# Token-major pieces on one PSUM bank of either pool, and longer pauses in the compression and the solve

## The chip, the cores and the metric

The kernel runs on one core of a Trainium2 chip. The time is that of the device for one execution, in microseconds (us); three executions give 573.76, 575.64 and 576.48, median 575.64. One more execution was profiled. The engines are PE (TensorE, the matmuls), PEld (its weight loads), DVE (VectorE), ACT (ScalarE), POOL (GpSimd) and SP (SyncE, which here only issues DMA transfers).

## The reference

One decoder layer for 256 tokens of width 2048. One input projection feeds eight heads of native sparse attention (NSA) and sixteen heads of RWKV-7 time mixing; their gated outputs go through one output projection, a norm and the residual. Cut to what matters here:

```python
def compress(kv, pos, w1, w2):          # called for k_cmp and for v_cmp
    idx = jnp.arange(n_cmp)[:, None] * CMP_STRIDE + jnp.arange(CMP_BLOCK)[None, :]
    blocks = kv[:, idx] + pos[None, None, :, None, :]
    flat = blocks.transpose(0, 1, 3, 2, 4).reshape(B, n_cmp, G, CMP_BLOCK * D)
    return jax.nn.silu(flat @ w1) @ w2  # w1 is 4096 x 128
...
h = x + RMSNorm_post( W_out( concat[ NSA_heads * silu(z_A), RWKV7_heads * silu(z_B) ] ) )
```

## The kernel before

Everything is unrolled. **Projection pieces** are the bulk of PE's work. Each takes a weight tile by DMA (L276, tile `rf...`, `rt...` or `ro...` for feature-major, token-major and output pieces), is split into a high half by ACT (L284, `hf`, `ht`, `ho`) and a low half by DVE (L285, `lf`, `lt`, `lo`), and is multiplied in three products: high by high and low of x, low by high. Most have 24 matmuls of 128x256 per weight tile. The two token-major pieces (function `token_major`, w = 0 and 1) instead use x as the stationary operand: each accumulates two token halves, 128x268 each, over six weight tiles, `pts` being the two PSUM banks; ACT empties them at L1073 (values) and L1074 (gates).

**Lanes** are generators that run beside the pieces: `rwkv`, `blk0`, `blk1`, `nsa0`, `nsa1`, `gate`, `chain`. A lane does a step and yields a number; it is continued when the planned PE time `now` has passed by that number. So the yields decide where in the written order a step stands. A scheduler with priorities (fetch before chain, evac, rwkv, mix, proj) then sets the final order of every engine from the written one, and the order is fixed at build time. The program waits on the chip where an operand isn't ready when its engine gets to it.

**PSUM** has eight banks. `ppool` owns banks 0 and 1 (NPP = 2) and serves the projection pieces in turn; `banks` owns the other six and serves the lanes. SBUF work space is one arena of 51 units of 256 columns, given out by first fit.

**Compression.** `compress` runs for kc and vc in lane nsa0. The 2 MB of w1 come in four quarters of 512 KB (tile `arena<-in_cw_dram`; L878 loads the first, L882 the next one). Each quarter feeds 8 matmuls of 128x128 with four small stationary tiles; the next-but-one quarter can only be loaded when a quarter's slot in the arena is free again.

**Solve.** For each half of the RWKV heads `solve` inverts 32x32 triangles on DVE (L672 and L674), sends the result Z and its transpose to DRAM (`zs`, `zt`, L680 and L681) and back into other partitions (L694 and L701), and multiplies corners of 32x32 with them (the corner products, on GR and ZT). A loop over four chunks follows; its last step is a group of 8 matmuls on VS and GR and 4 on AR (yp), and ends half 1. Then: ACT copies and squares (L813, L823), DVE reduces (L824), ACT takes a root (L827, with a table load), DVE scales (L828, L829), PE transposes 16 tiles of 64x64 (L164, ytp), DVE adds (L839).

**Output.** Output piece `ho`nj multiplies the mixed heads of index j into output columns n. j = 0 to 3 are NSA's (tile mixA), j = 4 to 7 RWKV's (mixB, split by ACT L1040 and DVE L1041 per half; it takes the place of GR, so it begins when the last yp has read GR). L1048 gates a head before the split.

The function that this change touches, as the profile's line numbers have them:

Of the kernel before, what the change touches and what calls it, by code (L numbers as in the profile page):

```python
# [117 lines left out]
def hybrid_block(ctx: ExitStack, tc: tile.TileContext, xT, xtok, wfm, wtm, wout, vecs, gpost, lora, table,  # L118
# [15 lines left out]
    @contextmanager  # L134
    def at(name):
        old, tc.cur_priority = tc.cur_priority, level[name]
        try:
            yield
        finally:
            level[name], tc.cur_priority = tc.cur_priority, old  # L140
# [6 lines left out]
    def mm(o, lhsT, rhs, **kw):  # L147
        n = 1
        for d_ in rhs.shape[1:]:
            n *= d_  # L150
        now[0] += n * (1 if rhs.dtype == F32R else 4) / 2400.0
        last[0] = PE.matmul(o, lhsT, rhs, **kw)  # L152
# [25 lines left out]
    banks = Pool(lambda a, k: banks_[:, NPP + a, :] if k == 1 else banks_[:, NPP + a:NPP + a + k, :], 8 - NPP, now)  # L178
    ppool = Pool(lambda a, k: banks_[:, a, :], NPP, now)

    def sb(k=1):
        while arena.find(k) is None:
            yield lambda: arena.find(k) is not None
        return arena.take(k)

    def bank():
        while banks.find(1) is None:
            yield lambda: banks.find(1) is not None
        return banks.take(1)
# [6 lines left out]
    def bank2():  # L196
        while banks.find(2, 2) is None:
            yield lambda: banks.find(2, 2) is not None
        return banks.take(2, 2)
# [24 lines left out]
    def progress():  # L224
        go = True
        while go:
            go = False
            for n in lanes:
                if can(n) and running[n][0] <= now[0]:
                    step(n)  # L230
                    go = True
                    break
# [8 lines left out]
    def until(cond):  # L241
        while not cond():
            wait()

    def pick(pool, k, step_=1):
        until(lambda: pool.find(k, step_) is not None)
        return pool.take(k, step_)
# [60 lines left out]
    def take():  # L308
        while queue and len(ready) < 4:
            fetch()  # L310
        return ready.pop(0)
# [225 lines left out]
    def block(A, hb, i, m):  # L537
        yield lambda: A.opened and A.normed[i]
        yield from rwkv_k(A, i, m)
        yield from rwkv_r(A, i, m)  # L540
        yield from rwkv_v(A, i, m)
        A.blocks += 1
        if A.blocks == 4:
            lanes["chain"].append(solve(hb))
# [103 lines left out]
    def solve(hb):  # L648
# [49 lines left out]
        for par in range(2):  # L698
            b0 = 64 * (1 - par)
            for a in range(2):  # L700
                SP.dma_start(ZT[b0:b0 + 32, :, a, :], ztv[0, par, :, :, a])  # L701
        yield 9.0
        t2p = yield from bank2()
        t2v = t2p[:, :, 0:T].rearrange("p b (j a s) -> p b j a s", j=4, a=2)
        for i in range(4):
# [153 lines left out]
    def compress(a, nm):  # L859
        if a == 0:  # L860
            SP.dma_start(post, pos)
            SP.dma_start(w2t, cw2)
        blks = yield from sb(4)
        blk = blks.ap.rearrange("p (j g i) -> p j g i", j=32, g=2)
        POOL.memset(blk[:, :, :, 15:16], 0.0)
        src = cT[nm].ap
        for g in range(2):
            w_g = bass.AP(tensor=src.tensor, offset=src.offset + g * T, ap=[src.ap[0], [1, 32], [16, 15]])
            DVE.tensor_tensor(blk[:, :, g, 0:15], w_g, post[:, a, :, None].to_broadcast([P, 32, 15]), op=ALU.add)
        cT[nm].free(2.0)  # L870
        yield 1.0
        cps = yield from bank()
        w1n = None
        for hf in range(4):
            w1 = w1n
            if w1 is None:
                w1 = yield from sb(4)
                SP.dma_start(w1[:], cw1[a, :, 8 * hf:8 * hf + 8, :].rearrange("p j d -> p (j d)"))  # L878
                yield 3.0
            if hf < 3:  # L880
                w1n = yield from sb(4)
                SP.dma_start(w1n[:], cw1[a, :, 8 * hf + 8:8 * hf + 16, :].rearrange("p j d -> p (j d)"))  # L882
            for j in range(2):
                for q in range(4):
                    jj = 4 * j + q
                    mm(cps[32 * q:32 * q + 32, 0:P], blk[:, 8 * hf + jj].rearrange("p g i -> p (g i)"),
                       w1[:, jj * P:jj * P + P], start=hf == 0 and j == 0, stop=hf == 3 and j == 1)
            w1.free(1.0)
            yield 2.0
        blks.free(1.0)  # L890
        csb = yield from sb()
        DVE.tensor_copy(csb[:, 0:P], cps[:, 0:P])
        cps.free(1.0)
        yps = yield from bank()
        mm(yps[:, 0:32], csb[:, 0:P], qsum, start=True, stop=True)
        csb.free(1.0)
        yh = tp.tile([P, 32], F32, tag="yh", name=f"yh{nm}")
        DVE.tensor_scalar(yh, yps[:, 0:32], 0.5, None, op0=ALU.mult)
        yps.free(1.0)
        yt = tp.tile([P, 32], F32, tag="yt", name=f"yt{nm}")  # L900
        ACT.activation(yt, yh, AF.Tanh)
        DVE.scalar_tensor_tensor(yh, yt, 1.0, yh, op0=ALU.add, op1=ALU.mult)
        yield 2.0
        ops = yield from bank()
        if a == 0:
            mm(ops[:, 0:32], w2t[:, a, :], yh, start=True, stop=True)
            for g in range(2):
                ACT.activation(KCH[:, g, 128:144], ops[:, 16 * g:16 * g + 16], AF.Copy)
                DVE.tensor_tensor(KCL[:, g, 128:144], ops[:, 16 * g:16 * g + 16], KCH[:, g, 128:144].bitcast(F32),
                                  op=ALU.subtract)  # L910
        else:
            for g in range(2):
                mm(ops[0:16, g * P:(g + 1) * P], yh[:, 16 * g:16 * g + 16], w2t[:, a, :], start=True, stop=True)
            opv = ops[0:16, 0:2 * P].rearrange("p (g d) -> p g d", g=2)
            ACT.activation(vcS[0:16], opv, AF.Copy)
            ACT.activation(vcS[64:80], opv, AF.Copy)
            DVE.tensor_tensor(vcS[32:48], opv, vcS[0:16].bitcast(F32), op=ALU.subtract)
        ops.free(2.0)
        ready_kv[nm] = True
        yield 0.4  # L920
# [132 lines left out]
    def token_major():  # L1053
        VV = N_.VV = pick(arena, 4).ap.rearrange("p (w i t) -> p w i t", w=2, i=2)
        for w in range(2):
            pts = [pick(ppool, 1) for i in range(2)]
            for hf in range(len(TMK) - 1):
                H, L = take()
                with at("proj"):
                    for part in range(2):  # L1060
                        for k in range(TMK[hf + 1] - TMK[hf]):
                            kk_ = TMK[hf] + k
                            for i in range(2):
                                xs = slice(i * P, (i + 1) * P)
                                if part == 0:
                                    mm(pts[i][:, 0:268], xH[:, kk_, xs], H[:, k, :], start=kk_ == 0, stop=False)
                                    mm(pts[i][:, 0:268], xL[:, kk_, xs], H[:, k, :], start=False, stop=False)
                                else:
                                    mm(pts[i][:, 0:268], xH[:, kk_, xs], L[:, k, :], start=False, stop=kk_ == NK - 1)
                progress()  # L1070
            with at("evac"):
                for i in range(2):
                    ACT.activation(VV[:, w, i, :], pts[i][:, 0:T], AF.Copy, scale=rst[:, i:i + 1])  # L1073
                    ACT.activation(gate[:, i, 12 * w:12 * w + 12], pts[i][:, T:268], AF.Tanh, scale=rsth[:, i:i + 1])  # L1074
                    pts[i].free(1.0)
        DVE.tensor_scalar(gate, gate, 0.5, 0.5, op0=ALU.mult, op1=ALU.add)
        ready_kv["tm"] = True
# [6 lines left out]
    for j, (nm, i) in enumerate(FM):  # L1084
        if j == N_PRE_TM:
            token_major()
# [27 lines left out]
        elif nm in ("kc", "vc"):  # L1114
# [5 lines left out]
            if i == 1:  # L1120
                lanes["nsa0"].append(compress(("kc", "vc").index(nm), nm))
# [45 lines left out]
    def out_part(n, js, pool, order=None):  # L1167
        pts = [pick(pool, 1) for i in range(2)]
        for pair in order or [[j] for j in js]:
            hl = [take() for j in pair]  # L1170
            for i in range(2):
                with at("proj"):
                    for j, (H, L) in zip(pair, hl):
                        out_mms(pts[i][:], i, H, L, j, j == js[0], j == js[-1])
            progress()
        return pts

    for n in range(NA):
        pts = out_part(n, range(4), ppool if n % 2 == 0 else banks)
# [51 lines left out]
    for n in range(4):  # L1231
# [7 lines left out]
        pts = out_part(n, js, ppool if n % 2 == 0 else banks, order)  # L1239
# [85 lines left out]
```

## Time and profile before

| | |
|---|---|
| three timed runs, median | 573.76, 575.64, 576.48 us; 575.64 us |
| the profiled execution's own time | 576.96 us |
| its span, first to last instruction | 575.2 us |
| PE busy, PEld busy | 557.7 us (97%), 522.1 us (91%) |
| DVE, ACT, POOL busy | 426.9 us (74%), 311.7 us (54%), 57.4 us (10%) |
| mean granted TensorE clock | 0.992 |

The span is what the trace covers; 1.76 us of the own time lie around it. Busy is the time in which an engine has an instruction in it. A matmul's end is modelled and overlaps the next one's start, so the distance from start to start says more than a duration. In a list by time, the square bracket behind an instruction gives the idle time ahead of it and what ended it.

### The profile page before, as it was taken

Reading aid. Unit: us, or ns where it says so; the run is one execution under the profiler, and the core shown is the slowest. Engines: PE = TensorE matmul, PEld = TensorE weight load, DVE = VectorE, ACT = ScalarE, POOL = GpSimd, SP = SyncE. Lnnn points to the kernel's source line nnn. Section 1 sums busy time; section 2 is a strip of 40 time slices with the busy share of each in tenths; the row PEclk is TensorE's granted clock in tenths of the full one; section 3 lists DMA queues with packets and bytes.
Section 4 is the critical chain, followed back from the end, with each engine's and each line's share of the span. In section 5 each row is a group of like instructions: output and inputs, shape, how many; then the busy total and the mean of one; then the engine's idle time right before and its main releaser. Section 6 shows DMA issues by size and latency. Waiting matters only on the chain.

```text
span 575.2 us, 12152 instructions
## 1 busy us (share of the span) xinstructions
PE 557.7 (97%) x4808; PEld 522.1 (91%) x4808; DVE 426.9 (74%) x885; ACT 311.7 (54%) x561; POOL 57.4 (10%) x97
## 2 busy tenths in 40 slices
PE   7999999999989999999998999999999999999993
PEld 7999999989989999999998999999999987778882
DVE  5989978859968765578759569999666566666755
ACT  7678656524436334476655667865543355645432
POOL 5103303300010000030102000000000000000002
PEclk9999999999989999999999999999999999999998
DMA  8796554477556734344256454434754446756624
GB/s 309 289 289 211 165 179 148 146 212 231 181 185 199 199 128 144 111 148 117 53 186 199 141 141 148 144 121 147 212 148 153 141 150 186 287 183 204 198 74 147
DMA packets 40789, 99.97 MB, mean 174 GB/s; under 512 B 14331, under 2 KB 17052, under 8 KB 40348
## 3 DMA queue, kind: packets, MB, share of 16 engines
q1 hardware_dynamic: 40444, 98.88, 53.9%
q8 instruction: 38, 0.62, 0.4%
q10 hardware_dynamic: 288, 0.31, 0.2%
q14 instruction: 19, 0.16, 0.1%
HBM read 93.93 MB, written 5.24 MB: 172 GB/s over the span
## 4 chain that ended last, share of the span: by engine, by line
PE 88%; DMA 5%; ACT 3%; SPq 1%; DVE 1%; issue 1%; POOL 0%; DVEq 0%; ACTq 0%; POOLq 0%
PE banks L152 86%; DMA arena<-in_cw_dram 2%; PE banks L164 2%; DMA xr<-in_xT_dram 1%; DMA arena<-zt 1%; SPq L694 1%; DMA zs<-arena 1%; DMA rt__3359<-in_wtm_dram 1%; DVE y L1222 0%; POOL xH L326 0%; ACT L559 0%; ACT L827 0%; SPq L276 0%; ACT hf__2850 L284 0%; ACT hf__3585 L284 0%
## 5 line engine op out<-in xcount | busy, mean ns | idle before, releaser
L152 PE MATMUL banks<-arena 128*32 128x128 f32 (+4 forms) x468 | 31.9, 256 | 3.0 <-DMA arena<-in_cw_dram 1.9
L152 PEld LDWEIGHTS banks<-arena 128*32 128x32 f32 (+3 forms) x468 | 26.4, 136 | 6.5 <-DMA arena<-in_cw_dram 2.6
L672 DVE TENSOR_TENSOR arena<-arena 64x31 f32<-64x31 f32 (+15 forms) x62 | 20.3, 328 | 6.3 <-DMA arena<-us 5.7
L674 DVE TENSOR_TENSOR arena<-arena 64x31 f32<-64x31 f32 (+15 forms) x62 | 20.5, 331 | 0.5
L473 ACT ACTIVATE small<-small 128x256 f32<-128x256 f32 x25 | 12.5, 507 | 14.9 <-DVE small L471 14.8
L164 PE MATMUL banks<-small,arena 128*128 128x128 f32 (+1 forms) x112 | 16.1, 262 | 0.0
L528 DVE RECIPROCAL arena<-arena 128x256 f32<-128x256 f32 x8 | 14.0, 1746 | 2.6 <-PE banks L152 2.6
L152 PE MATMUL banks<-AR,arena 64*128 64x128 f32 x128 | 14.3, 292 | 0.0
L1029 ACT ACTIVATE arena<-arena 128x256 f32<-128x256 f32 x16 | 6.6, 414 | 13.9 <-DVE arena L1141 9.8
L971 ACT ACTIVATE arena<-arena,mx 128x128 f32<-128x128 f32 (+1 forms) x32 | 14.1, 444 | 0.0
L558 POOL TENSOR_SCALAR arena<-arena 128x256 f32<-128x256 f32 x8 | 8.6, 1076 | 54.7 <-ACT arena L557 51.6
L164 PEld LDWEIGHTS banks<-small,arena 128*128 128x128 f32 (+1 forms) x112 | 12.0, 140 | 1.9 <-issue 1.1
L152 PEld LDWEIGHTS banks<-AR,arena 64*128 64x128 f32 x128 | 11.4, 187 | 2.2 <-issue 0.8
L1226 POOL TENSOR_TENSOR y<-y,xres 128x512 f32<-128x512 f32 x2 | 2.9, 1453 | 105.0 <-ACT y L1225 105.0
L474 DVE SCALAR_TENSOR_TENSOR arena<-small 128x256 f32<-128x256 f32 x25 | 12.0, 480 | 1.0 <-ACT small L473 0.8
L621 DVE TENSOR_TENSOR GR<-banks,small 128x1024 f32<-128x1024 f32 x8 | 9.8, 1220 | 3.8 <-PE banks L152 3.7
L152 PE MATMUL banks<-VS,GR 128*64 128x64 f32 x256 | 11.4, 229 | 0.0
L561 POOL TENSOR_SCALAR arena<-arena,small 128x256 f32<-128x256 f32 x8 | 6.1, 757 | 50.9 <-ACT arena L559 50.8
L585 POOL COPY AR<-arena 128x4 f32<-128x4 f32 x8 | 8.6, 1078 | 24.7 <-DVE arena L575 24.7
L152 PEld LDWEIGHTS banks<-VS,GR 128*64 128x64 f32 x256 | 9.6, 137 | 1.7 <-issue 0.4
L795 POOL MEMSET arena<- 64x256 f32 x12 | 3.7, 307 | 69.1 <-PE banks L152 66.1
L471 DVE TENSOR_TENSOR small<-banks,small 128x256 f32<-128x256 f32 x25 | 10.3, 418 | 0.1
(1378 smaller groups left out, 2157.0 us busy)
## 6 DMA issues: line engine op xcount, KB each, us to landing
arena<-in_cw_dram SPq DMA_DIRECT2D x8, 512.0 KB, 6.2
xres<-in_xtok_dram SPq DMA_DIRECT2D x2, 1024.0 KB, 10.1
xr<-in_xT_dram SPq DMA_DIRECT2D x3, 512.0 KB, 9.0
bscr<-arena SPq DMA_DIRECT2D x1, 1536.0 KB, 8.7
out_dram<-y SPq DMA_DIRECT2D x5, 256.0 KB, 3.1
arena<-bscr SPq DMA_DIRECT2D x8, 128.0 KB, 2.9
gpt<-in_gpost_dram SPq DMA_DIRECT2D x1, 1024.0 KB, 6.8
rf__93<-in_wfm_dram SPq DMA_DIRECT2D x1, 512.0 KB, 4.7
```

The costliest lines, as they stand in the source:

```text
L152: last[0] = PE.matmul(o, lhsT, rhs, **kw)
L164: PE.transpose(out=o, in_=i, identity=idn)
L471: DVE.tensor_tensor(f[:, 1:T + 1], pt[:, :T], rbc, op=ALU.mult)
L473: ACT.activation(tm, f[:, 0:T], AF.Copy, scale=vcol(V_MU, c))
L474: DVE.scalar_tensor_tensor(o, f[:, 1:T + 1], omu[:, c:c + 1], tm, op0=ALU.mult, op1=ALU.add)
L528: pace(DVE.reciprocal(A.nrm[i + j], A.nrm[i + j]))
L558: POOL.tensor_scalar(u[:], u[:], 1.0, None, op0=ALU.add)
L585: POOL.tensor_copy(A.AR[:, i, :, 0, 0:1], kk4[:, :, 0:1])
L621: DVE.tensor_tensor(A.GR[:, i].rearrange("p h c t -> p (h c) t"), gp.ap.rearrange("p h (c t) -> p (h c) t", c=4), gmask[:, None, :].to_bro ...
L672: DVE.tensor_tensor(t_, U[:, 0:j, j:j + 1].to_broadcast([64, j, w]), Z[:, j:j + 1, j:32].to_broadcast([64, j, w]), op=ALU.mult)
L674: DVE.tensor_tensor(Z[:, 0:j, j:32], Z[:, 0:j, j:32], t_, op=ALU.add)
L971: ACT.activation(dst, dst, AF.Exp, bias=mx[:, i, j:j + 1], accum_out=sm[:, i, j:j + 1])
```

## The change

Three numbers and one allocation. In `solve` the pause between the return loads of ZT and the corner products grows from 9 to 11. In `compress` the pause behind the first quarter's load grows from 3 to 6, and that behind each quarter's matmuls from 2 to 5. A token-major piece takes one bank from `ppool` and one from the lanes' `banks` where it took both from `ppool`. A blank line is added, so lines above 1055 are one higher afterwards.

```diff
@@ solve @@
                 SP.dma_start(ZT[b0:b0 + 32, :, a, :], ztv[0, par, :, :, a])
-        yield 9.0
+        yield 11.0
         t2p = yield from bank2()
@@ compress @@
                 SP.dma_start(w1[:], cw1[a, :, 8 * hf:8 * hf + 8, :].rearrange("p j d -> p (j d)"))
-                yield 3.0
+                yield 6.0
...
             w1.free(1.0)
-            yield 2.0
+            yield 5.0
@@ token_major @@
         for w in range(2):
-            pts = [pick(ppool, 1) for i in range(2)]
+
+            pts = [pick(ppool, 1), pick(banks, 1)]
```

Since the lanes' slots in the arena and the pauses decide what is written when, the order of all engines shifts from the first compression on. Three places follow.

SP's queue around the two middle quarters of kc's compression, before (`rf` are weight tiles of pieces, `us` belongs to the solve of half 0):

```order
L276 DMA rf171__1446<-in_wfm_dram 128x1024
L276 DMA rf180__1480<-in_wfm_dram 128x1024
L659 DMA us0_1510<-GR0_730 32x16x32 x4
L276 DMA rf181__1528<-in_wfm_dram 128x1024
L665 DMA arena_73<-us0_1510 64x1024
L882 DMA arena_73<-in_cw1_dram 128x1024 x2
L276 DMA rf190__1569<-in_wfm_dram 128x1024
L276 DMA rf191__1617<-in_wfm_dram 128x1024
L878 DMA arena_73<-in_cw1_dram 128x1024
L882 DMA arena_73<-in_cw1_dram 128x1024
```

And after:

```order
L276 DMA rf171__1446<-in_wfm_dram 128x1024
L276 DMA rf180__1480<-in_wfm_dram 128x1024
L882 DMA arena_73<-in_cw1_dram 128x1024
L659 DMA us0_1510<-GR0_730 32x16x32 x4
L276 DMA rf181__1519<-in_wfm_dram 128x1024
L882 DMA arena_73<-in_cw1_dram 128x1024
L665 DMA arena_73<-us0_1510 64x1024
L276 DMA rf190__1558<-in_wfm_dram 128x1024
L276 DMA rf191__1595<-in_wfm_dram 128x1024
L927 DMA arena_73<-bscr_301 128x256
L878 DMA arena_73<-in_cw1_dram 128x1024
```

The two L882 loads stood back to back behind the us transfers; now one is issued two weight tiles' places earlier, ahead of us, and the other by itself between.

PE around the last yp step of half 1, before (`ho`, `lo` are output pieces):

```order
L152 MATMUL banks_74<-ho03__5826,mixA_5805 128x512 x4
L152 MATMUL banks_74<-lo03__5825,mixA_5805 128x512 x2
L152 MATMUL banks_74<-VS1_3318,GR1_3317 64x64 x8
L152 MATMUL banks_74<-arena_73,AR1_3316 64x128 x4
L152 MATMUL banks_74<-ho10__5857,mixA_5805 128x512 x4
L152 MATMUL banks_74<-lo10__5856,mixA_5805 128x512 x2
L152 MATMUL banks_74<-ho11__5884,mixA_5805 128x512 x4
L152 MATMUL banks_74<-lo11__5883,mixA_5805 128x512 x2
```

And after:

```order
L152 MATMUL banks_74<-VS1_3336,GR1_3335 64x64 x8
L152 MATMUL banks_74<-arena_73,AR1_3334 64x128 x4
L152 MATMUL banks_74<-ho04__6039,mixB_6006 128x512 x7
L152 MATMUL banks_74<-lo04__6038,mixB_6006 128x512 x2
L152 MATMUL banks_74<-ho04__6039,mixB_6006 128x512
L152 MATMUL banks_74<-lo04__6038,mixB_6006 128x512 x2
L152 MATMUL banks_74<-ho05__6065,mixB_6006 128x512 x7
L152 MATMUL banks_74<-lo05__6064,mixB_6006 128x512 x2
L152 MATMUL banks_74<-ho05__6065,mixB_6006 128x512
L152 MATMUL banks_74<-lo05__6064,mixB_6006 128x512 x2
L164 MATMUL banks_74<-small_72,arena_73 128x64 x12
L152 MATMUL banks_74<-ho14__6159,mixB_6006 128x512 x4
```

Before, 44 matmuls on mixA stood between yp and the first group of transposes (L164), and pieces on mixB came later still. Now the pieces on mixA are all done ahead of yp, 24 matmuls on mixB stand behind it, and then twelve of the sixteen transposes.

ACT at the same place, before:

```order
L1182 ACTIVATE y2_5822<-banks_74 128x512
L284 ACTIVATE ho13__5941<-ro13__5938 128x1024
L1182 ACTIVATE y2_5822<-banks_74 128x512
L1040 ACTIVATE mixB_5932<-arena_73 128x256 x4
L813 ACTIVATE arena_73<-banks_74 128x256
L823 ACTIVATE arena_73<-arena_73 128x1024
L827 ACT_TABLE_LOAD
L827 ACTIVATE small_72<-small_72 128x16
L284 ACTIVATE ho20__5965<-ro20__5962 128x1024
```

And after (L1183 is the former L1182):

```order
L1183 ACTIVATE y2_5747<-banks_74 128x512
L284 ACTIVATE ho07__6141<-ro07__6138 128x1024
L1183 ACTIVATE y2_5747<-banks_74 128x512
L1040 ACTIVATE mixB_6006<-arena_73 128x256 x4
L813 ACTIVATE arena_73<-banks_74 128x256
L823 ACTIVATE arena_73<-arena_73 128x1024
L284 ACTIVATE ho14__6159<-ro14__6156 128x1024
L827 ACT_TABLE_LOAD
L827 ACTIVATE small_72<-small_72 128x16
L284 ACTIVATE ho15__6177<-ro15__6174 128x1024
L1040 ACTIVATE mixB_6006<-arena_73 128x256 x4
```

The chain L1040, L813, L823, table load, root now has a cast (`ho14`) ahead of the table load, and a cast (`ho07`) between the two evictions ahead of L1040; the second four L1040 follow closely.

Two further places in words. In vc's compression 43 matmuls of 128x256 stood between the second and the third quarter, and 46 stand there now; both loads are still issued together. In kc's compression 41 stood there and 33 do now. The corner products of half 0 still come in two parts of 1 and 15 with weight pieces between.

## Rows read from the trace of the kernel before

**Rows 1.** The page: span, and busy time, share and instructions of the engines.
```profile
span 575.2 us, 12152 instructions
PE 557.7 (97%) x4808; PEld 522.1 (91%) x4808; DVE 426.9 (74%) x885; ACT 311.7 (54%) x561; POOL 57.4 (10%) x97
```
**Rows 2.** Waits of PE: instruction, what it waited for, us in total, times, longest.
```profile
PE banks L152 <- ACT small L1074: 2.8, 2, 1.6
PE banks L152 <- DMA arena<-in_cw_dram: 1.9, 2, 1.4
...
PE banks L152 <- DMA arena<-zt: 0.6, 1, 0.6
```
**Rows 3.** PE by time, behind each token-major piece: start, us, engine, line, operation.
```profile
298.49 0.39 PE L152 MATMUL banks<-ht__3293,xH 128*128 128x268 f32 x1 [1.19 <-ACT small L1074]
...
313.74 0.39 PE L152 MATMUL banks<-xH,hf__3520 128*128 128x256 f32 x1 [1.59 <-ACT small L1074]
```
**Rows 4.** ACT by time at the same two places.
```profile
297.04 0.87 ACT L284 ACTIVATE ht__3415<-rt__3412 128x804 fp32r<-128x804 f32 x1
...
298.18 0.26 ACT L1074 ACTIVATE small<-banks,small 128x12 f32<-128x12 f32 x1
...
312.13 1.04 ACT L284 ACTIVATE hf__3628<-rf__3625 128x1024 fp32r<-128x1024 f32 x1
...
313.43 0.26 ACT L1074 ACTIVATE small<-banks,small 128x12 f32<-128x12 f32 x1
```
**Rows 5.** PE by time in the compressions of kc and vc.
```profile
128.28 0.62 PE L152 MATMUL banks<-arena 128*32 128x128 f32 x10 [0.49 <-DMA arena<-in_cw_dram]
...
163.91 0.28 PE L152 MATMUL banks<-xL,hf__1814 128*128 128x256 f32 x1
165.62 0.64 PE L152 MATMUL banks<-arena 128*32 128x128 f32 x16 [1.43 <-DMA arena<-in_cw_dram]
...
168.50 1.91 PE L152 MATMUL banks<-xH,lf__1813 128*128 128x256 f32 x8
170.21 0.42 PE L152 MATMUL banks<-xH,hf__1849 128*128 128x256 f32 x1
```
**Rows 6.** SP by time: issues of the third and fourth quarters.
```profile
122.31 0.83 SPq L882 DMA_DIRECT2D arena<-in_cw_dram  x2
...
158.47 0.80 SPq L882 DMA_DIRECT2D arena<-in_cw_dram  x2
```
**Rows 7.** The tile in_cw_dram: us from issue to landing of its eight loads.
```profile
DMA to landing us min/median/max: 5.0/6.5/7.9
```
**Rows 8.** Stretches: us, busy us of the engines, granted clock (PEclk), DMA share, GB/s.
```profile
167.00:167.60 0.60, 0.60 (x16) 0.31 (x13) 0.00 (x0) 0.00 (x0) 0.55 (x2) 0.61 0.49 198
168.00:169.00 1.00, 1.00 (x6) 1.00 (x6) 0.68 (x3) 0.26 (x1) 0.82 (x3) 0.50 0.27 98
170.50:171.00 0.50, 0.50 (x6) 0.50 (x6) 0.50 (x1) 0.00 (x0) 0.00 (x0) 0.95 0.00 0
310.00:316.00 6.00, 4.41 (x45) 4.05 (x44) 5.69 (x12) 4.19 (x10) 1.58 (x2) 1.00 0.70 219
```
**Rows 9.** PE by time from the end of half 1's yp to the transposes.
```profile
487.46 1.19 PE L152 MATMUL banks<-ho__5857,mixA 128*128 128x512 f32 x4
...
497.66 0.46 PE L164 MATMUL banks<-small,arena 64*128 64x64 f32 x4
```
**Rows 10.** ACT by time: the split of mixB, and a cast that waits for its tile.
```profile
487.46 1.32 ACT L1040 ACTIVATE mixB<-arena 128x256 fp32r<-128x256 f32 x4
...
499.01 1.06 ACT L284 ACTIVATE ho__6017<-ro__6014 128x1024 fp32r<-128x1024 f32 x1 [2.90 <-DMA ro__6014<-in_wout_dram]
```
**Rows 11.** DVE by time: the scaling ahead of the transposes, a low half, the add behind the transposes.
```profile
492.09 1.23 DVE L829 TENSOR_TENSOR arena<-arena,small 128x1024 f32<-128x1024 f32 x1
...
496.92 1.23 DVE L285 TENSOR_TENSOR lo__5990<-ro__5988,ho__5991 128x1024 fp32r<-128x1024 f32 x1
498.16 0.48 DVE L839 SCALAR_TENSOR_TENSOR arena<-banks,small,arena 128x256 f32<-128x256 f32 x1
```

## The prediction

> **What bounds the kernel now.** I read the page first: PE holds an instruction for 557.7 of 575.2 us, and its weight loads for 522.1 [rows 1]. So PE is the bound, and since the change neither adds nor removes a matmul, only PE's waits, its clock and the ends of the span can move the time. Next the list of PE's waits: 2.8 us for the eviction of token-major banks, 1.9 us for w1 quarters, 0.6 us for the return of ZT [rows 2]. Those are just the places that the change touches, 5.3 us together, 0.9% of the span. Then the lists by time show what stands ahead of each, and last the granted clock in the stretches around them.
>
> The clock shows something that the list of waits hides. In vc's compression PE waits 1.43 us for the third quarter at 165.62 [rows 5]; from within 167.00 to 167.60 (0.61) to within 170.50 to 171.00 (0.95) the granted clock is at 0.50, the lower of its two levels, 1.2 GHz against 2.4 [rows 8]. With the first stretch at half clock for 0.47 us, 2.9 us between, and 0.05 us of the last, that is 3.4 us at half speed, so 1.7 us of matmul time lost. The rows by time agree: eight steps from 168.50 to 170.21 take 1.71 us [rows 5], 0.214 each, which is 0.107 at full clock. Not every wait does it: around the token-major wait of 1.59 us the clock stays at 1.00 [rows 3, 8].
>
> The profiled execution took 576.96 us, 575.2 of span and 1.76 around it, 1.32 above the median of 575.64. I sum on 576.96 and take the 1.32 off at the end. About 0.5%, 2.9 us, is what a measurement of this kernel can tell from no change.
>
> **Token-major banks.** Before, both pieces and the feature-major piece behind them use banks 0 and 1, so each starts when the one before has been evicted. The evictions are short (L1074 0.26 us), but ACT gets to them late: casts for later weight tiles stand ahead (0.87 us from 297.04; 1.04 us from 312.13), and PE goes on only when L1074 ends, 298.18 + 0.26 = 298.44 and 313.43 + 0.26 = 313.69 [rows 3, 4]. Afterwards piece 0 has one bank of each kind, piece 1 the other one and a further lane bank, and the next piece finds a `ppool` bank that had its eviction six weight tiles ago. Nothing is left to wait for: -1.19 - 1.59 = **-2.8 us**. The order of ACT there stays about as it was, so the eviction is as late as before, but what is late next is only a lane that wants this bank. The price is one of the six lane banks less for two pieces' time. If that bank is missed at every take and the wait is as long as the longest here, it is +1.59 once or twice; I take 0, since in the order the next user of the emptied lane bank stands some 35 matmuls behind. Bounds -2.8 to +0.4.
>
> **Compression.** What counts is not the pause but how much matmul work stands between the moment that a quarter's slot becomes free (then SP issues the load two quarters on) and the matmuls that want it. For kc, before, both loads are issued from 122.31 on, and PE stands for 0.49 us until 128.28 [rows 5, 6], so PE had 5.5 us of work and the load needed almost 6. After, 33 matmuls instead of 41 stand there, but the third quarter's load is issued by itself, ahead of the us transfers, when the first quarter's matmuls are done and the second's still run, which gives some 4.9 us. A load needs 5.0 to 7.9 us from issue to landing, 6.5 in the median [rows 7]; alone it should be near the 5.0. So a wait of 0.1 up to 1.6 us is left against 0.49: I take 0.5, that is **0** (-0.4 to +1.1). The fourth quarter has 4.4 us more of work ahead of it and should be in time.
>
> For vc both loads are issued from 158.47 on, PE is at the third quarter after 43 matmuls, 163.91 + 0.1 - 158.47 = 5.5 us later, and starts at 165.62, 7.15 us after the issue [rows 5, 6]. After, 46 matmuls give 46/43 of that, 5.9 us. With 6.5 us to landing the wait is about 0.7, with the old 7.15 it is 1.3, with 5.0 none: I take 0.7, **-0.7 us** (-1.4 to 0; 7.9 us to landing would give 2.0, so +0.6).
>
> **The clock behind vc.** The token-major wait of 1.59 us left the clock alone, the 1.43 us in the midst of small matmuls did not. With half the wait I take it that the clock stays up: **-1.7 us**, or 0 if it falls again. The Trainium skill has a rule on this, in "TensorE: Matmul & The Clock Gate", "What's actually happening": the clock of the array is halved when PE has been idle lately, and given back once it has been busy. By that rule the waits that this change leaves or makes can cost more than their length; were the clock to fall once more behind a new wait, the sum would be 1.7 us higher. The trace agrees behind vc's wait (0.50) and not behind the token-major one (1.00).
>
> **Corner products.** The wait of 0.6 us [rows 2] is for a chain: Z to DRAM, back in eight loads, then ZT in four on the same SP queue. All of that moves back together with the corner products, behind weight tiles whose loads now stand between the parts of the chain on SP. Two more units of pause are 2 us of matmul work at most, and I see the queue take about as much. **0**, from -0.6 (gone) to +0.6 (doubled). Half 1's loads land long before their use in both orders.
>
> **The end of half 1, which the diff doesn't name.** Since the compression and the first solve come later, everything behind them in the lanes does, and the last yp now stands directly ahead of the first pieces on mixB. Call the end of yp E; before it is 487.46, when the next piece starts and ACT begins L1040 [rows 9, 10]. Then the chain of ACT and DVE runs to the end of L829 at 492.09 + 1.23 = 493.32 [rows 11], E + 5.9, and PE comes to the transposes at 497.66 after 44 matmuls, E + 10.2 [rows 9], 0.232 each. So there were 4.3 us to spare. After, 24 matmuls stand between, E + 5.6, and the chain has a cast of 1.04 us (the size in [rows 4]) ahead of its table load: E + 6.9. PE loses about 1.35 us, part of it at `ho04`, which must wait for the first L1040 and L1041. Then `ho06` wants the second half of mixB: by the time the transposes begin DVE has a low half (1.23, as in [rows 11]), some five adds and gatings and one L1041 ahead (each about 0.48), together 4.1 us, while PE has 12 transposes (0.46 for four [rows 9], 1.4) and 10 matmuls (2.3), 3.7 us; with the adds waiting for the transposes' ends I count 0.55 more. Together **+1.9 us**. Below: the cast waits for no one and runs early, 0.3; above: a cast that waits for its tile, as one did for 2.90 us [rows 10], comes ahead of the chain: +2.9 and more.
>
> **Sum.** -2.8 + 0 - 0.7 - 1.7 + 0 + 1.9 = -3.3 us: 573.7 on the profiled execution's own time, **572.3 us** on the median's.
>
> **Rivals.** *A, the compression is not eased (the change doesn't do what it says there).* The scheduler and the load decide, not the pauses: vc's wait stays at 1.4 us and the clock falls behind it. For it: 3 matmuls more is little, and the loads still go out in a pair. -2.8 + 1.9 = -0.9: 574.7.
> *B, the end costs nothing.* ACT runs the cast ahead while yp is still on, or the first pieces on mixB have slack that I don't see. Against it: the order of ACT is fixed and the chain has no gap to give. -2.8 - 0.7 - 1.7 = -5.2: 570.4.
> *C, slower.* At the end ACT's casts, `ho14` ahead of the table load and `ho15` ahead of the second L1040, each wait for their tiles 2.9 us, as in [rows 10]. PE then stands 1.35 + 2.9 ahead of the transposes and 0.55 + 2.9 at `ho06`, 7.7 us, and with the clock down behind them 9.4: +4.2, 579.8. It decides once the end costs over 8.1 us instead of 1.9. For it: the tiles' buffers come free only as PE goes on; against: of the waits before, none of this kind reached PE.
> *D, the clock falls behind the end's waits*, as it did behind vc's, though those 1.9 us are spread over two or three waits: 572.3 + 1.7 = 574.0. This is the case that the rule on the clock speaks for.
>
> **How the numbers follow.** My forecast 0.38, A 0.24, B 0.18, C 0.10, D 0.10. The bound for faster is 572.8, for slower 578.5. My forecast's own range is 570.5 to 574.3, with the corner's and kc's bounds in it, so a little over half of it is faster (0.21); B nearly all (0.17); A and D by small margins (0.06 of 0.34). That gives faster 0.44, C slower and a little from kc's and the lane bank's upper bounds 0.11, the rest, 0.45, no difference. The range goes from B less 0.9 (the corner wait gone too) to A plus kc's and vc's upper bounds: 569.5 to 577.3. It leaves out C and the far side of B.
>
> **What would show it.** Right: no PE wait for L1073 or L1074 left; one wait for w1 of under 1 us in vc with the clock at 1.00 behind it; a new wait of PE at `ho04` and at the L164 transposes behind the last yp, about 1.4 us together, and at `ho06` about 0.5. Wrong: a clock at 0.50 behind vc or behind the transposes, waits of lanes' matmuls for a bank around the token-major pieces, a wait for zt over 1 us, or ACT idle for a `ro` tile between yp and the transposes.

## The result, and the profile after

The changed kernel is slower: 577.71 us, median of 13 runs (576.74 to 581.37), against 575.16 of before in the same comparison; the ratio of the comparison is 1.0076, interval 1.0058 to 1.0093 (the two medians alone give 1.0044). Two more comparisons of the same two kernels gave 1.0063 (1.0034 to 1.0093) and 1.0052 (1.0029 to 1.0076). The forecast was 572.3, range 569.5 to 577.3.

The profiled execution took 576.74 us, the lowest of its runs, where the one of before (576.96) lay above all 13 of its own. So the two pages look alike (span 575.0 us against 575.2, PE busy for 558.6 us against 557.7), and the difference has to be found by stage. Of PE's waits after, those for w1 and for zt (instruction, what it waited for, us in total, times, longest):

```profile
PE banks L152 <- DMA arena<-in_cw_dram: 1.4, 2, 0.9
...
PE banks L152 <- DMA arena<-zt: 0.6, 3, 0.2
```

The waits for L1074 of [rows 2, 3] are gone. The one for w1 is smaller. For zt there are three waits now, and three new ones stand at the end of half 1: for L1040, L829 and L839. PE there, by time, from the start of the last yp:

```profile
504.87 0.73 PE L152 MATMUL banks<-VS,GR 128*64 128x64 f32 x16
...
506.42 1.89 PE L152 MATMUL banks<-ho__6039,mixB 128*128 128x512 f32 x7 [0.38 <-ACT mixB L1040]
...
513.34 0.47 PE L164 MATMUL banks<-small,arena 64*128 64x64 f32 x8 [1.15 <-DVE arena L829]
514.87 0.46 PE L164 MATMUL banks<-small,arena 64*128 64x64 f32 x4 [1.06 <-DVE arena L839]
```

ACT at the same place:

```profile
509.05 1.06 ACT L284 ACTIVATE ho__6159<-ro__6156 128x1024 fp32r<-128x1024 f32 x1 [0.40 <-PE banks L152]
510.13 1.28 ACT L827 ACT_TABLE_LOAD   x1
```

and DVE:

```profile
512.05 1.23 DVE L829 TENSOR_TENSOR arena<-arena,small 128x1024 f32<-128x1024 f32 x1
513.20 1.22 DVE L285 TENSOR_TENSOR lo__6158<-ro__6156,ho__6159 128x1024 fp32r<-128x1024 f32 x1
514.33 0.87 DVE L839 SCALAR_TENSOR_TENSOR arena<-banks,small,arena 128x256 f32<-128x256 f32 x2
```

The cast of `ho14` stands ahead of the table load, as the order said, and the transposes start when L829 ends (512.05 + 1.23 = 513.28). The second wait was not foreseen: the third group of transposes needs a bank that L839 must empty, and on DVE the low half `lo14` stands ahead of L839 (513.20, 1.22 us). Then the clock falls. Stretches after, columns as in [rows 8]:

```profile
515.00:516.00 1.00, 0.98 (x6) 0.81 (x6) 1.00 (x4) 0.37 (x1) 0.00 (x0) 0.82 0.65 123
516.00:519.00 3.00, 3.00 (x8) 2.34 (x7) 1.87 (x5) 0.86 (x3) 0.00 (x0) 0.50 0.39 156
```

In vc's compression the wait of 1.43 us [rows 5] is 0.56 now, and the clock stays at 1.00 there (185 to 190 us):

```profile
186.12 0.64 PE L152 MATMUL banks<-arena 128*32 128x128 f32 x16 [0.56 <-DMA arena<-in_cw_dram]
```

The corner products of half 0 changed too, which the section on the change has wrong. The trace counts each of these matmuls twice, so x62 is 31 of them. Before, they came in parts of 1 and 31; the larger one:

```profile
194.39 1.16 PE L152 MATMUL banks<-arena,GR 32*32 32x32 f32 x62 [0.55 <-DMA arena<-zt]
```

Afterwards they come in four parts of 1, 15, 1 and 15, with weight pieces between; the two larger ones:

```profile
204.25 0.83 PE L152 MATMUL banks<-arena,GR 32*32 32x32 f32 x30
...
206.49 0.83 PE L152 MATMUL banks<-arena,GR 32*32 32x32 f32 x30 [0.15 <-DMA arena<-zt]
```

**By stage.** From all matmul starts of a trace one can work out PE's lag: the start of a matmul less the sum of the usual steps (the median from start to start, by shape) of all matmuls ahead of it. Where it grows, PE waits, changes kind or runs at the low clock, whatever the order. Two executions of before, three of the changed kernel, and the two last experiments, us, at the time in the head:

```
time            110    160    190    220    290    320    500    end
before        11.04  15.75  20.35  21.40  22.76  25.45  31.67  32.63
before (e8)   11.17  15.68  18.99  19.60  20.92  23.71  29.92  30.89
changed       11.11  15.41  18.28  20.66  22.39  22.72  27.85  33.06
changed (e7)  11.19  15.70  17.93  22.48  24.31  24.57  29.85  33.56
changed (e12) 11.32  16.17  18.40  21.04  22.87  23.21  28.98  34.11
e13           11.20  15.97  18.20  18.81  20.84  20.83  26.33  29.90
e14           10.57  15.17  17.76  18.38  20.41  20.40  27.15  28.56
```

The changed kernel against before, means: nothing to 160 us (kc); -1.5 from 160 to 190 (vc and the clock behind it); **+2.4 from 190 to 220** (corner products of half 0); +0.5 to 290; -2.4 from 290 to 320 (token-major); -0.8 to 500; **+3.7 from 500 to the end**. At 500 us it is 1.9 ahead, at the end 1.8 behind. (In before the end of half 1 lies ahead of 500 us; PE waits for nothing there.)

### The profile page after: what moved, and what is told of

Same layout as the page of the kernel before. It is cut to its first block, busy times and chain, and to the rows that moved or that the text cites. A ratio compares the mean times of both kernels' runs of the same rounds, so it can differ in the third digit from the quotient of the medians.

```text
span 575.0 us, 12169 instructions
## 1 busy us (share of the span) xinstructions
PE 558.6 (97%) x4808; PEld 522.5 (91%) x4808; DVE 428.8 (75%) x885; ACT 311.6 (54%) x561; POOL 57.7 (10%) x97
## 4 chain that ended last, share of the span: by engine, by line
PE 90%; DMA 5%; ACT 2%; DVE 1%; issue 1%; SPq 1%; DVEq 0%; ACTq 0%
PE banks L152 87%; DMA arena<-in_cw_dram 2%; PE banks L164 2%; DMA rf__2416<-in_wfm_dram 1%; DMA rf__93<-in_wfm_dram 1%; DMA arena<-zt 1%; ACT L827 0%; DVE y L1223 0%; SPq L659 0%; ACT L571 0%; DVE lf__2267 L285 0%; DVE lo__6158 L285 0%; ACT hf__115 L284 0%; ACT ho__6141 L284 0%; SPq L276 0%
## 5 line engine op out<-in xcount | busy, mean ns | idle before, releaser
L164 PE MATMUL banks<-small,arena 128*128 128x128 f32 (+1 forms) x112 | 16.8, 263 | 2.2 <-DVE arena L829 1.1
L152 PE MATMUL banks<-AR,arena 64*128 64x128 f32 x128 | 15.8, 287 | 0.0
L164 PEld LDWEIGHTS banks<-small,arena 128*128 128x128 f32 (+1 forms) x112 | 11.7, 140 | 3.9 <-DVE arena L829 1.6
L152 PEld LDWEIGHTS banks<-AR,arena 64*128 64x128 f32 x128 | 12.9, 187 | 2.2 <-issue 0.5
L585 POOL COPY AR<-arena 128x4 f32<-128x4 f32 x8 | 7.3, 913 | 63.8 <-DVE arena L575 63.8
L687 POOL MEMSET arena<- 32x512 f32 x4 | 2.1, 519 | 95.8 <-PE banks L152 62.5
L561 POOL TENSOR_SCALAR arena<-arena,small 128x256 f32<-128x256 f32 x8 | 7.6, 952 | 38.4 <-ACT arena L559 38.3
```

Source lines behind the costliest of these rows:

```text
L164: PE.transpose(out=o, in_=i, identity=idn)
L561: POOL.tensor_scalar(fk[:], ta[:], ka2[:, m:m + 1], ka1[:, m:m + 1], op0=ALU.mult, op1=ALU.add)
L585: POOL.tensor_copy(A.AR[:, i, :, 0, 0:1], kk4[:, :, 0:1])
```

## The experiments

All ratios are to before in the same comparison, with intervals.

**e1 to e4: parts of the change.** e1 has the bank hunk alone:

```diff
-            pts = [pick(ppool, 1) for i in range(2)]
+            pts = [pick(ppool, 1), pick(banks, 1)]
```

e2 has the three pauses alone, e3 the bank and the compression's pauses, e4 the bank and the solve's pause:

```diff
# e2, e3
-                yield 3.0
+                yield 6.0
-            yield 2.0
+            yield 5.0
# e2, e4
-        yield 9.0
+        yield 11.0
```

e1: 

> Only the token-major pieces' banks are changed; all pauses stay as before, and with them the end of half 1 (44 matmuls stand again between the last yp and the first transposes). Theory E (the changed kernel lost its gain at the end of half 1, where the profile after shows PE waits of 0.4, 1.1 and 1.1 us and a granted clock of 0.50 behind them): the two waits of 1.19 and 1.59 us vanish and nothing comes in their place, so about 3 us faster than before, 572.2 on 575.2, ratio 0.995. Theory S (the lane bank that is taken away is the cost): as slow as the changed kernel, 577 to 578, with new waits of lanes' matmuls near the token-major pieces.

e2: 

> The three pauses are changed, the token-major pieces keep both banks of their own pool. Theory E: the end of half 1 stands as in the changed kernel (24 matmuls on mixB between the last yp and the transposes), so its waits and the low clock behind them come, some 4.8 us, and the bank gain of 3 us is missing: 3 us slower than the changed kernel, about 580.5, ratio to before 1.009 to 1.013. Theory S: no bank is taken, so no slower than before, 575 to 576.

e3: 

> The banks and the compression's pauses are changed, the solve's pause stays 9. The last yp stands 5 us of matmuls later than before, and 13 us of matmuls follow ahead of the first transposes, against the 7 us that the chain needs. Theory E: no wait at the end, so 572 to 573; what vc's compression gains or loses in wait and clock shows by itself (573 if the clock falls there, 571.5 if it does not). Theory S: 577 to 578.

e4: 

> The banks and the solve's pause are changed, the compression's pauses stay 3 and 2. The last yp stands 11 us later than before, and 11.6 us of matmuls follow ahead of the first transposes. Theory E: no wait at the end, so 572 to 573, as with the banks alone, with vc's wait of 1.4 us and its low clock as before. Theory S: 577 to 578.

Measured: e1 574.48, 0.9999 (0.9976 to 1.0022); e2 577.89, 1.0047 (1.0023 to 1.0070); e3 576.24, 1.0023 (1.0001 to 1.0044); e4 576.51, 1.0020 (1.0003 to 1.0038). Theory S falls: the bank alone costs nothing, and e2, without it, is about as slow as the changed kernel. But theory E isn't simply right either: e2 is not 3 us slower than the changed kernel, and e1, e3 and e4 have no wait at the end and still don't gain the 3 us. In e1 the two waits for L1074 vanish, and two others come 20 us behind the pieces, at 332 and 338 us, for lane banks that DVE empties:

```profile
PE banks L152 <- DVE GR L621: 0.7, 1, 0.7
PE banks L152 <- DVE arena L635: 0.6, 1, 0.6
```

Its lag grows by -0.1 us from 290 to 320 (20.38 to 20.24), against 2.7 before, and then by 4.2 from 320 to 340 (to 24.41), against 1.4. So the gain was made and given back. e3 shows the same two waits (0.6 and 0.7). In e4 PE waits 3.4 us for w1, in two waits, and the granted clock is at 0.66 from 130 to 135 us, behind the first of them. e2 has the three waits at the end as in the changed kernel (0.4, 1.2, 1.1) and the clock at 0.61 from 515 to 520. The order tells why only the two sets of pauses together do it: the last yp stands 5 us of matmuls later with the compression's pauses alone, 11 with the solve's alone, 22 with both.

**e5, e11: the end repaired. e6: another way to it.**

```diff
# e5, e11, on the changed kernel
-        yield 11.0
+        yield 9.0 if hb else 11.0
# e6, on the changed kernel
-            yield ZLAT
+            yield (0.7 if hb else ZLAT)
```

e5: 

> The changed kernel, with the solve's pause back at 9 for half 1 alone. PE's order is that of the changed kernel up to the corner products of half 1; from there the last yp stands 16 us of matmuls earlier, and 11.4 us of matmuls lie between it and the first transposes. Theory E (the gain is lost at the end of half 1): PE's waits of 0.4, 1.1 and 1.1 us at the first piece on mixB and at the transposes vanish, and the granted clock stays up there; some 4 us faster than the changed kernel, 573.5, and 0.995 to 1.000 of before. Theory R (the end is not special; the changed order loses a little everywhere, or the clock falls elsewhere in most executions): within 1 us of the changed kernel, 577 to 578, ratio to before 1.004 or more.

e11: 

> The changed kernel with the pause of 9 for half 1, once more, on the same chip as the two above and the changed kernel: 574 to 574.5 again, 4 us below the changed kernel.

e6: 

> The changed kernel, with the pause between the 31 steps of half 1's triangle inversion 0.7 instead of 1.0. The order is that of the changed kernel up to half 1's inversion; the last yp stands where it stood before the change, 10.7 us of matmuls ahead of the transposes. Theory E: as with the pause of 9, no wait at the end and no low clock, 573.5, unless DVE gets to the inversion's steps too late and PE waits for the corner products' loads of half 1 instead. Theory R: 577 to 578.

e5 took 574.09, 0.9987 (0.9964 to 1.0010), and e11 576.27, 0.9998 (0.9973 to 1.0022), beside 1.0063 and 1.0052 for the changed kernel in the same comparisons (e7, e12): 5 to 8 parts in a thousand, 3 to 4.4 us, from one pause, with PE's order the same up to 442 us. No wait is left at the end in either. By its own median e11 missed what was expected of it, 574 to 574.5. e6 failed: 577.81, 1.0041 (1.0016 to 1.0067). Its last yp stands early and no wait is left at the transposes, but now the lane's own chain holds PE ahead of them (0.8 us for L796, and 1.3 at yp), and in its profile the clock is at 0.53 from 205 to 210 us, behind the corner products. So its whole time doesn't test the end:

```profile
PE banks L152 <- DVE VS L769: 1.3, 1, 1.3
```

**e7, e8, e12: the same kernels again.**

e7: 

> The changed kernel as it is, in another execution. Theory E: the waits at the end recur with the same sizes (0.4, 1.1, 1.1 us), since they come from the order, and the clock is at 0.50 behind them again; median 577 to 578. Theory R: these waits or the clock there vary from execution to execution, and other stretches show the low clock.

e12: 

> The changed kernel, a third execution under the profiler, on the same chip: 577.5 to 579. Waits of 0.6, 1.3 and 1.2 us of start-to-start time at the end as twice before; the corner products of half 0 wait 0.6 to 1.6 us, and the clock falls behind one or the other of them.

e8: 

> The kernel before as it is, in another execution. If the low clock behind vc's compression and the two waits for L1074 (1.2 and 1.6 us) belong to the kernel, they recur, and the time is near 575 to 577. If the low clock is a matter of the single execution, the time is 1.7 us less, 573 to 575, with the waits as before; if the waits too vary, the change's gain at the banks was overstated from one profile.

e7 took 579.01, 1.0063; e12 577.91, 1.0052; e8, one run, 574.84. The waits at the end came with the same sizes in all three executions of the changed kernel (first transposes 8.47, 8.45 and 8.45 us behind the start of the last yp). The clock did not: low behind the end in two of three, and in e7 behind the corner products instead. e7's PE at the corner:

```profile
206.32 0.22 PE L152 MATMUL banks<-arena,GR 32*32 32x32 f32 x2 [1.46 <-DMA arena<-zt]
```

and e7's stretches there and at the end, with the granted clock ahead of the DMA share (0.83 and 1.00):

```profile
205.00:210.00 5.00, 3.68 (x47) 3.49 (x48) 2.40 (x4) 0.00 (x0) 0.00 (x0) 0.83 0.29 102
...
517.00:520.00 3.00, 2.98 (x15) 2.47 (x16) 2.85 (x8) 1.23 (x3) 0.00 (x0) 1.00 0.73 240
```

e8 repeats the waits for L1074 of before, but not the low clock behind vc's wait, which [rows 8] had shown. e8's waits of PE:

```profile
PE banks L152 <- ACT small L1074: 2.9, 2, 1.7
...
PE banks L152 <- DMA arena<-in_cw_dram: 1.3, 1, 1.3
```

and e8's stretch behind vc, at 1.00:

```profile
165.00:170.00 5.00, 4.50 (x57) 3.90 (x58) 3.13 (x8) 2.28 (x4) 2.27 (x6) 1.00 0.45 169
```

**e9: work added into the wait**, in the changed kernel, of no use to the result:

```diff
             ytp = yield from bank()
+            if hb and i == 0:
+                for q in range(16):
+                    mm(ytp[:, :T], late[0][:, 0, 0:P], late[0][:, 0, :], start=True, stop=True)
```

> The changed kernel with 16 matmuls of 128x256 added that compute nothing of use (mixA by mixA into the bank that the first transposes then overwrite). In the order they stand between the last yp and the first piece on mixB, 16 x 0.12 = 1.9 us of work, just where PE waits 0.6 and, ahead of the transposes, 1.3 us. Theory E (the chain of ACT and DVE sets when the transposes can start): the added work fits into the waits, so the time is that of the changed kernel within 0.5 us, or up to 1.7 us less where it keeps the clock up; the waits for L1040 and L829 are gone. Theory R (the chain isn't what holds PE there): 1.9 us slower.

579.12, 1.0067 (1.0044 to 1.0090), beside 1.0052 (1.0029 to 1.0076) for the changed kernel in the same comparison. PE by time:

```profile
507.00 0.73 PE L152 MATMUL banks<-VS,GR 128*64 128x64 f32 x16
...
508.10 2.18 PE L152 MATMUL banks<-mixA 128*128 128x256 f32 x16
...
515.68 0.47 PE L164 MATMUL banks<-small,arena 64*128 64x64 f32 x8
517.52 0.46 PE L164 MATMUL banks<-small,arena 64*128 64x64 f32 x4 [1.37 <-DVE arena L842]
```

The first transposes start 515.68 - 507.00 = 8.68 us behind the start of the last yp, against 513.34 - 504.87 = 8.47 in the changed kernel: 1.9 us of work cost 0.2, and the waits for L1040 and L829 are gone. That settles the chain as what holds PE there. The second wait stays (L842 is the former L839), and the clock falls behind it all the same (0.50 at 519 to 522 us), so filling the first wait didn't keep it up in this execution. It fell behind e9's corner products as well (0.83 from 205 to 210 us, as in e7). As for the whole time, 0.0015 more than the changed kernel lies within the intervals.

**e10: e5 with the old banks.**

```diff
-            pts = [pick(ppool, 1), pick(banks, 1)]
+            pts = [pick(ppool, 1) for i in range(2)]
```

> The compression's pauses, the solve's pause of 11 for half 0 and 9 for half 1, and the token-major pieces on their own two banks as before. 11.6 us of matmuls lie ahead of the first transposes, so no wait at the end. If the lane bank is worth what the profile of before said (the waits of 1.2 and 1.6 us for L1074), this is 2.8 us slower than the run with the lane bank (e11), near 577. If the gain at the banks is given back in the same stretch by the lanes, as between the kernel before and e1 and between e2 and the changed kernel, it is within 1 us of e11, near 574.5.

575.97, 1.0014 (0.9993 to 1.0035), beside e11's 0.9998: 0.9 us, within the intervals, so neither case is shown. In this order PE waits for L1074 (L1075 in e10's numbering) once, for 1.0 us, not twice.

**e13, e14: the return loads together.** `top` is a new level of priority ahead of all others. e13 is the changed kernel with this edit, e14 has the pause of 9 for half 1 as well:

```diff
-        SP.dma_start(zs, Z)
-        SP.dma_start(zt, U)
+        with at("top"):
+            SP.dma_start(zs, Z)
+            SP.dma_start(zt, U)
...
-                    SP.dma_start(ZBv[b0:b0 + 32, a, :, 32 * d:32 * d + 32], zsv[d, mp, :, a])
+                    with at("top"):
+                        SP.dma_start(ZBv[b0:b0 + 32, a, :, 32 * d:32 * d + 32], zsv[d, mp, :, a])
...
-                SP.dma_start(ZT[b0:b0 + 32, :, a, :], ztv[0, par, :, :, a])
+                with at("top"):
+                    SP.dma_start(ZT[b0:b0 + 32, :, a, :], ztv[0, par, :, :, a])
```

e13: 

> The changed kernel with one more edit: the twelve loads that bring Z and its transpose back (L694, L701) stand together on SP ahead of the next weight tiles, where the changed kernel has weight tiles between them; the corner products of half 0 then come in parts of 1 and 31 instead of 1, 15, 1 and 15. The end of half 1 stands as in the changed kernel. If these loads' place on SP made the changed kernel's wait at the corner products (0.6 to 1.6 us in three profiles, 2.4 to 4.6 us of PE's time from 190 to 220 us against 0.6 to 1.0 before), about 2 us faster than the changed kernel, 576, ratio to before 1.002. If that wait is only how the DMA happens to land, no change: 578, ratio 1.006.

e14: 

> Both repairs: the return loads together ahead of the weight tiles, and the solve's pause of 9 for half 1 (11.6 us of matmuls ahead of the first transposes). If the end of half 1 costs 3 to 4 us and the corner products 2 us, and the two add up: 572 to 573, ratio to before 0.995, faster than both kernels. If only the end counts: 574.5 to 575, ratio 0.999.

SP by time before, with two weight tiles among the twelve loads:

```profile
183.59 3.06 SPq L694 DMA_DIRECT2D arena<-zs  x5
186.69 0.45 SPq L276 DMA_DIRECT2D rf__2255<-in_wfm_dram  x1
187.18 1.42 SPq L694 DMA_DIRECT2D arena<-zs  x3
188.69 0.39 SPq L701 DMA_DIRECT2D arena<-zt  x1
189.20 0.38 SPq L276 DMA_DIRECT2D rf__2287<-in_wfm_dram  x1
189.63 1.41 SPq L701 DMA_DIRECT2D arena<-zt  x3
```

in the changed kernel, with two as well, but in other places, so that the loads of ZT are cut two and two:

```profile
195.06 1.82 SPq L694 DMA_DIRECT2D arena<-zs  x4
196.98 0.39 SPq L276 DMA_DIRECT2D rf__2416<-in_wfm_dram  x1
197.42 2.70 SPq L694 DMA_DIRECT2D arena<-zs  x4
200.22 0.89 SPq L701 DMA_DIRECT2D arena<-zt  x2
201.21 0.38 SPq L276 DMA_DIRECT2D rf__2456<-in_wfm_dram  x1
202.50 0.80 SPq L701 DMA_DIRECT2D arena<-zt  x2
```

and in e13 (L696 and L704 are L694 and L701):

```profile
194.92 4.59 SPq L696 DMA_DIRECT2D arena<-zs  x8
199.61 1.88 SPq L704 DMA_DIRECT2D arena<-zt  x4
201.59 0.38 SPq L276 DMA_DIRECT2D rf__2416<-in_wfm_dram  x1
```

The last load goes out at 201.5 instead of 203.3, the corner products come in parts of 1 and 31, PE waits for none of it, and the lag from 190 to 220 grows by 0.6 us instead of 2.4 to 4.6. e13: 575.56, 0.9989 (0.9969 to 1.0009), though its three waits at the end stand as in the changed kernel (0.4, 1.1, 1.1). That is more than the 2 us that were expected of it; in its profile the clock stayed at 1.00 behind these waits. e14: **572.38, 0.9951 (0.9929 to 0.9973)**, faster than before, and below the changed kernel's ratio in every comparison. Its transposes start 12.2 us behind the last yp and wait for nothing:

```profile
493.08 0.73 PE L152 MATMUL banks<-VS,GR 128*64 128x64 f32 x16
...
505.29 0.46 PE L164 MATMUL banks<-small,arena 64*128 64x64 f32 x4
```

Two losses, two repairs. The changed kernel was not run in this last comparison; against its 1.0052 to 1.0076 in the others e13 is 6 to 9 parts in a thousand lower, e14 10 to 13, and e5 and e11 were 5 to 8 lower than the changed kernel beside them. So they add up, as far as the intervals tell.

**All traces at the corner products.** Worked out as in the table, the lag from 190 to 220 us grows by 0.5 to 1.1 us in the nine executions with parts of 1 and 31 (before, e8, e1 to e4, e10, e13, e14) and by more in the seven with four parts: 2.4 to 2.7 where the clock stayed at 1.00 there (two of the changed kernel's three, e5, e11), 3.8 to 5.6 where it fell (e6, e7, e9). Before, e2 and e10 have two weight tiles among the twelve loads, just as the changed kernel has. So weight tiles there are not the cost by themselves; what goes with it is the cut into four parts, with waits for the later loads of ZT. e13 moves the loads and joins the parts in one edit, so which of the two counts for how much is not shown. And each pair of the three hunks (e2, e3, e4) keeps 1 and 31: only all three together make the four parts.

## Why the prediction was wrong

By stage the forecast was -3.3 and the traces give +1.8. Of the difference of 5.1 us the corner products make 2.4 and the end of half 1 makes 1.8; vc with its clock makes 0.9, the banks 0.4, and small terms take 0.3 back. Two of the prediction's own signs of being wrong came: the clock at 0.50 behind the transposes, and a wait for zt of over 1 us (1.46 in e7, 1.06 in e12).

- **The end of half 1 (+1.9): right mechanism, mis-sized.** It measured +3.7 over before. The first part was good: 1.35 was forecast to the transposes, 0.6 + 1.3 = 1.9 came from start to start. Missed was the wait for L839 in place of the one at `ho06`: 1.2 us. I had counted `lo14` ahead of the adds, but let only `ho06` pay for it, not the third group of transposes, which needs a bank that the first add empties. And the clock fell behind it in two of three executions, some 1.5 us each, as rival D had it. Rival C's place was right and its mechanism wrong: no cast waited for its tile.
- **Corner products (0, bounds -0.6 to +0.6): the step that failed.** I wrote that everything moves back together and took the longer pause to cover it. They didn't: the corner products went from two parts to four, which I had read as two still, and a weight tile cut the loads of ZT two and two instead of one and three. Weight tiles as such were no news on SP: two stood among these loads before as well. It measured +2.4, of which 1.7 is left by the two executions whose clock stayed up there (2.4 and 2.6 against 0.8 before). e13 shows that the place of these loads, with the parts on PE that follow from it, makes it. The longer pause did not cover it.
- **The clock behind vc (-1.7): half right.** The clock stayed up in the changed kernel, as forecast, but e8 shows that before doesn't always lose it either. A state of one execution was counted as the kernel's, and its price was too high: the usual step of a 128x256 matmul is 0.12 us in these traces, not 0.107, so 3.4 us at 0.214 a step lose 1.5, not 1.7. The Trainium skill's rule in "TensorE: Matmul & The Clock Gate", "What's actually happening", that idleness halves the clock, holds here as a risk: after the same waits at the end the trace shows 0.50 twice and 1.00 once.
- **vc's wait (-0.7): right**, 1.43 to 0.56 in the profiled execution, and none in e7 and e12. **kc (0): right in the lag** (nothing to 160 us), though the single wait for w1 is longer: 0.9, 1.1 and 1.4 us in the changed kernel, 0.3 to 1.6 in all eleven executions of this order, 0.5 and none before, within the bounds.
- **The banks (-2.8): right where they stand** (-2.4), but not shown to be worth that to the kernel: e1 gave it back by 340 us, and between e10 and e11 it is 0.9, within the intervals.
- **The sum.** -2.4 - 1.5 + 2.4 + 3.7 and small terms are +1.8 by these five traces; the comparisons say 3 to 4.4. Where the other executions lost the rest no trace shows; this part stays open. The mean granted clock (0.988 over the changed kernel's 13 runs, 0.991 over 34 of before beside e1 to e4) doesn't settle it, since it depends on what is on record of the start: from 8 to 14 us e12 shows 0.50 and the first profile of the changed kernel 1.00, with means of 0.987 and 0.993, though a step of 128x256 takes 0.21 us there in both.
- **The range.** Its ends don't come out of the terms that it names: B with the corner wait gone is 570.4 - 0.6 = 569.8, and A with kc's +1.1 and vc's +0.6 is 576.4. The measured 577.71 lies above either upper end.

## What to carry to other kernels

A pause or a bank that is changed in one place moves the whole order, so a wait that vanishes is only half of the sum: look for each long chain across engines (here yp, square, root, scale, transpose) and count how much of the bound engine's work still stands between its start and its end. In a chain through DRAM, see what else stands on the queue between its transfers, and into how many parts the work is cut that waits for them: putting the transfers together, which also joined the parts, was worth about as much here as the shorter pause for half 1. And compare several executions by stage before a low clock in one of them enters a sum.

## What had not been expected of the hardware

The granted clock at one and the same place varies from execution to execution of the same kernel. Behind vc's compression it was 0.50 in one execution of before and 1.00 in another, with waits of 1.43 and 1.32 us; at the end of the changed kernel 0.50, 1.00 and (516 to 519 us of e12) 0.54, with the three waits equal to 0.01 us. e2 and e13 have the same three waits, and the clock behind them was low in e2 (0.61 from 515 to 520 us) and at 1.00 in e13. The record of the clock is not complete either: where it shows 1.00 in the first 14 us of the changed kernel, PE's steps are those of the low clock. Single runs of one kernel spread over 3 to 8 us.
